# Shared pages in a recurrence without output, an identity with its own place, a new order, and a final layer norm on one engine

## The chip, the core and the metric

The kernel runs on one core of a Trainium2 chip. The metric is the device time of one execution in microseconds (us); the change is judged by the median of several executions of the kernel before and after.

## What is computed

Two layers of a block over an image stream x (512 tokens) and a context c (256 tokens), 1024 wide, in fp32. Each layer mixes a modulated input by four mixers, adds the result to the stream with a layer norm, and then does the same with a gated feed-forward. In the last layer c is only needed for the final states of its recurrence. Cut to what matters:

```python
for l in range(DEPTH):                       # 2
    last = l == DEPTH - 1
    hx, hc = xs * (1 + sc1) + sh1, cs * (1 + csc1) + csh1
    px = split(hx @ w_in[l])                 # rwkv, pool, gmlp, fnet columns
    pc = split(hc @ w_in[l][:, :RWKV_COLS]) if last else split(hc @ w_in[l])
    yc_f, sc_f = rwkv_scan(prep_c, 0, s0)    # S = S*w + (S @ -kk)(kk*a) + v k ; y = S @ r
    yc_b, sc_b = rwkv_scan(prep_c, 1, s0)
    yx_f, _ = rwkv_scan(prep_x, 0, sc_f)     # x starts from the final states of c
    yx_b, _ = rwkv_scan(prep_x, 1, sc_b)
    xs = layer_norm(ALPHA * xs + g1 * mix_out(px, yx_f, yx_b), ln1_g[l], ln1_b[l])
    xs = layer_norm(ALPHA * xs + g2 * swiglu(xs * (1 + sc2) + sh2), ln2_g[l], ln2_b[l])
    if not last:
        cs = the same two steps for c        # yc_f, yc_b are used here alone
return xs
```

## The kernel before

**Tiles.** A stream is kept in tiles of 128 tokens, x in four and c in two, each as two pages. A page is 128 partitions x 512 fp32; there are 63 of them, 12 half pages, 4 buffers (`raw`) of 512 KB in which weights land, 6 for split weights (`w`) and 8 banks of accumulators (`ps`). A matrix product is done in three matmuls of a split operand (`mm3`); so a weight that has landed is rounded on ScalarE (`w<-raw`) and its remainder taken on VectorE (`w<-raw,w`). Tensors with features on the partitions are called hT; `hT_block` makes them by transposes against the identity `idn`.

**Program and order.** `main` (L1670) writes a straight program for two branches at a time: the recurrence of one stream (`rwkv`: `rwkv_kk`, `group`, `values`, `inverse`, `scan`, `readout`) beside the output projection and feed-forward of the other (`w_out`, `ffn`, with `proj` and `proj_tile`, then a layer norm and hT). Nothing is issued while this is written. `arrange` (L560) finds the dependences, gives each instruction a due time by a backward schedule, subtracts from it the number that the table `LEAD` has for the instruction's label (one number for each label, in the order in which the labels first appear; a label is the part of the program, as `rwkv/0/x/group`), and lays the instructions out by a list scheduler (`schedule`, L404) that respects the pools and uses three more numbers (`RULES`). `emit` then issues every instruction from one line, L547, so that all rows of the profile carry that line and are told apart by the tiles' names. Each engine runs its instructions strictly in the order laid out; SP issues all DMAs, in order too.

**The lines that the change touches.**
`setup` (L682) loads the constants. `idn`, the identity and two columns of ones, comes by a DMA whose label is that of all of the setup.
`group` (L1192) prepares one direction pair of two heads in a segment of 256 tokens. Per direction it takes two pages for the rows that read the state (`AR`) and two for those that write it (`KB`), one for each of the two heads e; each page is 128 x 4 x 128. With `need_y` both column halves are used; without, which is the case for c in layer 1 alone (`start_mix(1, c, False, False)`), only the 64 columns that the state needs.
`scan` (L1377) multiplies these with the running state W.
`done` in `main` (L1759) is the final layer norm of a tile of x, after the last residual: statistics, then for the left half page two VectorE steps (x - mean) * g and * r + b, for the right half page a column nb = -mean * r on VectorE, x * r + nb on ScalarE, and on GpSimd (POOL) a multiplication by g and an addition of b; then two DMAs to the output. The table's order makes tiles 2 and 0 the last two.

Of the kernel before, what the change touches and what calls it, by code (L numbers as in the profile page):

```python
# [259 lines left out]
def analyse(ops):  # L260
# [68 lines left out]
)  # L329
RULES = {"horizon": 38406.3531, "sticky": {"scalar": 3473.0577, "tensor": 114.6915}, "cold": 1.2436167775899638e+16}  # L330


def delay(o, s):

    return LATENCY.get((o.eng, s.eng), 100.0)


def latest(ops, prio):

    n = len(ops)  # L340
# [1561 lines left out]
```

## Time and profile before

| | before |
|---|---|
| median of 3 runs | 1856.9 us (1855.26 to 1860.04) |
| the profiled execution | 1855.08 us |
| its span | 1853.3 us |
| mean granted clock of TensorE | 0.976 |
| PE busy | 1727.6 us, 93% |
| VectorE (DVE) busy | 1037.0 us, 56% |
| ScalarE (ACT) busy | 622.0 us, 34% |
| GpSimd (POOL) busy | 500.5 us, 27% |

Busy is the time in which an engine works on an instruction; a granted clock of 1.00 is 2.4 GHz, 0.50 is 1.2 GHz. The chain of waits is followed back from the last instruction to what released it at each step. Idle time of an engine matters where PE waits for it, or after PE's last matmul.

### The profile page before, as it was taken

Reading aid. Unit: us, or ns where it says so; the run is one execution under the profiler, and the core shown is the slowest. Engines: PE = TensorE matmul, PEld = TensorE weight load, DVE = VectorE, ACT = ScalarE, POOL = GpSimd, SP = SyncE. Lnnn points to the kernel's source line nnn. Section 1 sums busy time; section 2 is a strip of 40 time slices with the busy share of each in tenths; the row PEclk is TensorE's granted clock in tenths of the full one; section 3 lists DMA queues with packets and bytes.
Section 4 is the critical chain, followed back from the end, with each engine's and each line's share of the span. In section 5 each row is a group of like instructions: output and inputs, shape, how many; then the busy total and the mean of one; then the engine's idle time right before and its main releaser. Section 6 shows DMA issues by size and latency. Waiting matters only on the chain.

```text
span 1853.3 us, 33955 instructions
## 1 busy us (share of the span) xinstructions
PE 1727.6 (93%) x13896; PEld 1329.2 (72%) x13896; DVE 1037.0 (56%) x2067; ACT 622.0 (34%) x1265; POOL 500.5 (27%) x525
## 2 busy tenths in 40 slices
PE   6998889799998998999999999988979899999996
PEld 4787755588685567777787777776755788888885
DVE  3465755831253369844744456778856843443445
ACT  2455353421112124433323231564622222222220
POOL 4113531320020245600110213323416451100015
PEclk9999999799999999999999999998999999999999
DMA  8531276233463742322222223212475132333321
GB/s 308 176 114 40 83 260 222 70 115 125 143 210 124 262 155 80 125 99 84 80 92 81 84 82 119 86 57 75 138 269 183 40 112 99 99 97 112 114 80 46
DMA packets 84923, 228.93 MB, mean 124 GB/s; under 512 B 8864, under 2 KB 10272, under 8 KB 84768
## 3 DMA queue, kind: packets, MB, share of 16 engines
q1 hardware_dynamic: 84768, 226.77, 37.0%
q8 instruction: 109, 1.79, 0.4%
q14 instruction: 46, 0.38, 0.1%
HBM read 220.44 MB, written 6.29 MB: 122 GB/s over the span
## 4 chain that ended last, share of the span: by engine, by line
PE 76%; DVE 13%; DMA 4%; ACT 3%; issue 2%; POOL 1%; SPq 0%; POOLq 0%; DVEq 0%; ACTq 0%
PE ps L547 76%; DVE page L547 8%; DMA raw<-in_wm_dram 2%; DVE w L547 1%; ACT page L547 1%; POOL page L547 1%; ACT L547 1%; DVE s L547 1%; DVE NR L547 1%; ACT half L547 1%; DVE half L547 1%; DMA raw<-in_w_out_dram 1%; DMA raw<-in_w_dram 1%; DMA page<-keepM 0%; DVE Nc L547 0%
## 5 line engine op out<-in xcount | busy, mean ns | idle before, releaser
L547 PE MATMUL ps<-page,w 128*128 128x512 f32 (+1 forms) x3456 | 774.8, 377 | 25.6 <-DVE page L547 12.3
L547 PEld LDWEIGHTS ps<-page,w 128*128 128x128 f32 x3456 | 602.0, 191 | 160.2 <-DVE page L547 14.6
L547 POOL TENSOR_TENSOR page<-page 128x512 f32<-128x512 f32 (+4 forms) x250 | 324.6, 1311 | 841.8 <-DVE page L547 685.1
L547 DVE TENSOR_TENSOR w<-raw,w 128x512 fp32r<-128x512 f32 (+2 forms) x368 | 287.0, 790 | 342.7 <-PE ps L547 276.1
L547 ACT ACTIVATE w<-raw 128x512 fp32r<-128x512 f32 (+1 forms) x368 | 223.5, 624 | 515.7 <-PE ps L547 423.5
L547 PE MATMUL ps<-w,page 128*128 128x512 f32 (+2 forms) x1344 | 299.0, 369 | 4.3 <-DVE w L547 2.8
L547 PEld LDWEIGHTS ps<-w,page 128*128 128x128 f32 x1344 | 229.8, 188 | 57.3 <-issue 7.5
L547 PE MATMUL ps<-page 32*32 32x32 f32 (+2 forms) x5640 | 220.3, 221 | 25.4 <-issue 13.3
L547 PEld LDWEIGHTS ps<-page 32*32 32x32 f32 (+2 forms) x5640 | 169.0, 122 | 86.8 <-issue 43.8
L547 DVE TENSOR_TENSOR page<-ps,page 128x512 f32<-128x512 f32 x222 | 150.5, 685 | 139.9 <-PE ps L547 114.9
L547 ACT ACTIVATE page<-ps 128x256 f32<-128x256 f32 (+6 forms) x297 | 113.7, 401 | 223.8 <-PE ps L547 208.4
L547 PE MATMUL ps<-page,raw 128*128 128x256 f32 x704 | 165.0, 388 | 0.0
L547 PEld LDWEIGHTS ps<-page,raw 128*128 128x128 f32 x704 | 133.8, 193 | 26.9 <-issue 8.5
L547 PE MATMUL ps<-raw,page 128*128 128x512 f32 x240 | 113.1, 603 | 5.3 <-DVE page L547 2.4
L547 DVE TENSOR_TENSOR page<-ps,cst 64x256 f32<-64x256 f32 (+2 forms) x148 | 73.6, 513 | 21.7 <-PE ps L547 19.7
L547 PEld LDWEIGHTS ps<-raw,page 128*128 128x128 f32 x240 | 43.2, 189 | 48.4 <-issue 41.2
L547 PE MATMUL ps<-raw,sc 128*32 128x256 f32 x768 | 60.3, 408 | 17.7 <-DMA raw<-in_wm_dram 8.8
L547 ACT ACT_TABLE_LOAD x57 | 73.1, 1283 | 6.2 <-PE ps L547 4.4
L547 PE MATMUL ps<-idn,page 128*128 128x128 f32 (+1 forms) x292 | 48.8, 305 | 12.7 <-DVE page L547 10.1
L547 POOL TENSOR_TENSOR page<-page,half 64x256 f32<-64x256 f32 (+1 forms) x50 | 43.0, 860 | 65.1 <-ACT half L547 26.4
L547 POOL TENSOR_TENSOR half<-page,half 128x256 f32<-128x256 f32 x24 | 20.1, 840 | 142.7 <-DVE half L547 77.6
L547 ACT ACTIVATE half<-ps 128x256 f32<-128x256 f32 x34 | 12.9, 383 | 130.6 <-PE ps L547 130.6
(126 smaller groups left out, 1247.4 us busy)
## 6 DMA issues: line engine op xcount, KB each, us to landing
raw<-in_w_dram SPq DMA_DIRECT2D x196, 512.0 KB, 3.7
raw<-in_wm_dram SPq DMA_DIRECT2D x96, 512.0 KB, 4.6
raw<-in_win_dram SPq DMA_DIRECT2D x38, 512.0 KB, 3.6
raw<-in_w_out_dram SPq DMA_DIRECT2D x24, 512.0 KB, 4.8
page<-in_rows_dram SPq DMA_DIRECT2D x23, 256.0 KB, 5.0
page<-in_x_dram SPq DMA_DIRECT2D x16, 256.0 KB, 6.4
raw<-in_wk_dram SPq DMA_DIRECT2D x8, 384.0 KB, 6.2
page<-keepM SPq DMA_DIRECT2D x12, 256.0 KB, 4.8
```

The source lines that it names most:

```text
L547: r = getattr(getattr(nc, o.eng), meth)(*[conv(x) for x in args], **{k: conv(x) for k, x in kw.items()})
```

## The change

Three things are changed. The pages `AR` and `KB` of the two heads become one page (128 x 2 x 4 x 64) for a recurrence without output, with the column offsets set to suit. The identity's DMA gets a label of its own. The final layer norm's right half is done by two VectorE steps, as the left one, for tiles 0 and 2; tiles 1 and 3 stay as they are. Beside this every number of `LEAD` (one more than before) and of `RULES` is new. Matmuls are the same in number and shape; there are two ScalarE and four GpSimd instructions fewer, and two VectorE instructions more.

```diff
-RULES = {"horizon": 38406.3531, "sticky": {"scalar": 3473.0577, "tensor": 114.6915}, "cold": 1.2436167775899638e+16}
+RULES = {"horizon": 38909.7984, "sticky": {"scalar": 2492.3179, "tensor": 11.8601}, "cold": 2.8962643435601404e+19}
...
         idn = self.const.tile([128, 130], F32, name="idn")
+        up, nc.lab = nc.lab, ("idn",)
         nc.sync.dma_start(out=idn, in_=self.I["idn"])
+        nc.lab = up
...
-            AR.append([self.page([128, 4, 128]) for _ in range(2)])
-            KB.append([self.page([128, 4, 128]) for _ in range(2)])
+            for V_ in (AR, KB):
+                if st.need_y:
+                    V_.append([self.page([128, 4, 128]) for _ in range(2)])
+                else:
+                    t = self.page([128, 2, 4, 64])
+                    V_.append([t[:, e] for e in range(2)])
...
-                self.tt(A[:, :, ca + 1:ca + 64], nl[o, :, 1:64], c3(Pt)[o, :, 0:63], ALU.mult)
-                self.cp(A[:, :, ca:ca + 1], nl[o, :, 0:1])
+                ba = ca if st.need_y else 0
+                self.tt(A[:, :, ba + 1:ba + 64], nl[o, :, 1:64], c3(Pt)[o, :, 0:63], ALU.mult)
+                self.cp(A[:, :, ba:ba + 1], nl[o, :, 0:1])
...
             self.stt(S[0], S[0], mean, rows[0], ALU.subtract, ALU.mult)
-            self.ts(nb, mean, r, -1.0, ALU.mult, ALU.mult)
-            self.act(S[1], S[1], AF.Identity, bias=nb, scale=r)
             self.stt(S[0], S[0], r, rows[2], ALU.mult, ALU.add)
-            self.tt(S[1], S[1], rows[1], ALU.mult, self.nc.gpsimd)
-            self.tt(S[1], S[1], rows[3], ALU.add, self.nc.gpsimd)
+            if i in (0, 2):
+                self.stt(S[1], S[1], mean, rows[1], ALU.subtract, ALU.mult)
+                self.stt(S[1], S[1], r, rows[3], ALU.mult, ALU.add)
+            else:
+                self.ts(nb, mean, r, -1.0, ALU.mult, ALU.mult)
+                self.act(S[1], S[1], AF.Identity, bias=nb, scale=r)
+                self.tt(S[1], S[1], rows[1], ALU.mult, self.nc.gpsimd)
+                self.tt(S[1], S[1], rows[3], ALU.add, self.nc.gpsimd)
```

The order of the instructions at three places follows, of the kernel before and after. A row is an engine's instruction with its output and inputs by the program's names (numbers distinguish buffers), the shape, and how many of the kind follow each other.

VectorE behind w_out of layer 0 for c. `BN_STATS s_3934` (before) and `s_3831` (after) are the statistics of the last context tile; the `page<-page,mv,rs` that follows is its normalisation. Before:

```order
L547 TENSOR_TENSOR page<-ps,cst 64x256 x2
L547 TENSOR_TENSOR page<-page 128x512
L547 BN_STATS s_3934<-page 128x6 x2
L547 TENSOR_TENSOR page<-page,cst 128x512
L547 BN_AGGR mv<-s_3934 128x2
L547 TENSOR_TENSOR page<-ps,cst 64x512
L547 TENSOR_SCALAR v_3942<-mv 128x1
L547 TENSOR_REDUCE Nc<-page 128x64
L547 TENSOR_SCALAR page<-page,mv,rs 128x512
```

After:

```order
L548 TENSOR_TENSOR page<-page 128x512
L548 TENSOR_SCALAR kkn<-kkn 128x8
L548 BN_STATS s_3831<-page 128x6
L548 TENSOR_SCALAR page<-page,mv,rs 128x512 x2
L548 BN_AGGR mv<-s_3831 128x2
L548 RECIPROCAL kkn<-kkn 128x8
L548 TENSOR_SCALAR v_3847<-mv 128x1
L548 COPY page<-kkn 128x512
L548 TENSOR_SCALAR page<-page,mv,rs 128x512 x2
L548 TENSOR_TENSOR page<-page,ps 128x512
L548 TENSOR_TENSOR page<-page,half 64x4x63 x4
L548 TENSOR_TENSOR BK<-half 128x4x64 x2
L548 TENSOR_TENSOR page<-ps,cst 64x256 x2
```

The masks (`ps,cst`), the product with a constant and the reduction (`Nc`) stood ahead of the normalisation and now stand behind it.

PE where layer 0 of x ends. `ps<-w,page` are products of the projection's earlier part, `ps<-page 128x512 x72` its last part and the four residual tiles, `ps<-idn,page` the transposes to hT, `ps<-page,w 128x256` the first products of layer 1. Before:

```order
L547 MATMUL ps<-w,page 128x512 x6
L547 MATMUL ps<-page,w 128x512 x12
L547 MATMUL ps<-w,page 128x512 x12
L547 MATMUL ps<-page 128x512 x72
L547 MATMUL ps<-idn,page 128x128 x8
L547 MATMUL ps<-page,w 128x256 x12
L547 MATMUL ps<-idn,page 128x128 x16
L547 MATMUL ps<-page,w 128x256 x6
```

After:

```order
L548 MATMUL ps<-w,page 128x512 x6
L548 MATMUL ps<-page,w 128x512 x12
L548 MATMUL ps<-w,page 128x512 x15
L548 MATMUL ps<-page 128x512 x72
L548 MATMUL ps<-w,page 128x512 x3
L548 MATMUL ps<-idn,page 128x128 x24
L548 MATMUL ps<-page,w 128x256 x30
```

Three matmuls of the earlier part now stand between the last residual tile and the transposes, and the transposes and first products are no longer interleaved.

GpSimd and VectorE at the end of the program; `rs` is the reciprocal deviation of a tile. GpSimd before, then after, and VectorE after:

```order
L547 TENSOR_TENSOR rs<-v_17377,nhalf 128x1
L547 TENSOR_TENSOR page<-page 128x512 x3
L547 TENSOR_TENSOR rs<-v_17432,nhalf 128x1
L547 TENSOR_TENSOR rs<-v_17444,nhalf 128x1
L547 TENSOR_TENSOR page<-page 128x512 x4
```

```order
L548 TENSOR_TENSOR rs<-v_17369,nhalf 128x1
L548 TENSOR_TENSOR page<-page 128x512 x3
L548 TENSOR_TENSOR rs<-v_17424,nhalf 128x1
L548 TENSOR_TENSOR rs<-v_17434,nhalf 128x1
```

```order
L548 SCALAR_TENSOR_TENSOR page<-page,mv 128x512
L548 BN_STATS s_17418<-page 128x6
L548 SCALAR_TENSOR_TENSOR page<-page,mv 128x512
L548 BN_AGGR mv<-s_17418 128x2
L548 SCALAR_TENSOR_TENSOR page<-page,rs 128x512
L548 TENSOR_SCALAR v_17434<-mv 128x1
L548 SCALAR_TENSOR_TENSOR page<-page,mv 128x512 x2
L548 SCALAR_TENSOR_TENSOR page<-page,rs 128x512 x3
```

The four GpSimd steps behind the last `rs` are gone, and VectorE takes seven scalar-tensor steps after its last statistics, where there were three.

## Rows read from the trace of the kernel before

**Rows 1.** The page: busy time of each engine, and the chain that ended last.

```profile
PE 1727.6 (93%) x13896; PEld 1329.2 (72%) x13896; DVE 1037.0 (56%) x2067; ACT 622.0 (34%) x1265; POOL 500.5 (27%) x525
...
PE 76%; DVE 13%; DMA 4%; ACT 3%; issue 2%; POOL 1%; SPq 0%; POOLq 0%; DVEq 0%; ACTq 0%
```

**Rows 2.** Stretches: length, busy time (count) per engine, clock, DMA share, GB/s.

```profile
0.00:46.00 46.00, 30.90 (x177) 20.98 (x181) 17.56 (x38) 13.38 (x25) 19.67 (x50) 1.00 0.90 310
...
787.00:1145.00 358.00, 351.33 (x2344) 278.78 (x2342) 178.86 (x305) 111.36 (x209) 50.89 (x50) 1.00 0.27 90
...
1480.00:1807.00 327.00, 327.00 (x1425) 265.22 (x1424) 144.29 (x213) 88.13 (x147) 55.29 (x40) 1.00 0.32 103
...
1839.40:1853.30 13.90, 0.00 (x0) 0.00 (x0) 6.65 (x14) 1.63 (x2) 8.72 (x8) 0.68 0.25 94
```

**Rows 3.** Timeline of PE, start: start, length, instruction, [idle before, releaser].

```profile
10.40 0.99 PE L547 MATMUL ps<-idn,half 128*128 128x2 f32 x4 [2.02 <-DMA idn<-in_idn_dram]
...
16.96 1.08 PE L547 MATMUL ps<-raw,sc 128*32 128x256 f32 x8 [2.39 <-DMA raw<-in_wm_dram]
...
20.73 2.06 PE L547 MATMUL ps<-half 128*128 128x128 f32 x8
```

**Rows 4.** Timeline, 344 to 356, and the stretch behind it.

```profile
344.50 1.88 PE L547 MATMUL ps<-page 128*128 128x512 f32 x4
...
354.14 1.06 DVE L547 TENSOR_REDUCE Nc<-page 128x64 f32<-128x512 f32 x1
354.30 0.56 POOL L547 TENSOR_TENSOR rs<-v,nhalf 128x1 f32<-128x1 f32 x1 [3.65 <-DVE v L547]
...
355.11 0.54 DVE L547 TENSOR_SCALAR page<-page,mv,rs 128x512 f32<-128x512 f32 x1
...
355.71 1.97 PE L547 MATMUL ps<-idn,page 128*128 128x128 f32 x8 [5.82 <-DVE page L547]
...
352.70:362.90 10.20, 6.57 (x23) 5.55 (x24) 9.92 (x42) 5.99 (x12) 0.86 (x2) 0.50 0.01 2
```

**Rows 5.** Layer 0 to layer 1 of x: the first transposes, and two stretches.

```profile
1161.39 1.10 PE L547 MATMUL ps<-idn,page 128*128 128x128 f32 x8
...
1161.40:1183.70 22.30, 19.76 (x106) 16.58 (x105) 15.38 (x40) 9.26 (x19) 8.42 (x11) 0.85 0.11 25
1165.10:1171.90 6.80, 6.10 (x26) 5.26 (x25) 6.03 (x16) 2.66 (x6) 2.00 (x3) 0.50 0.00 0
```

**Rows 6.** Groups by form (busy us, mean ns | idle before), then timeline at 1143.

```profile
L547 DVE TENSOR_TENSOR w<-raw,w 128x512 fp32r<-128x512 f32 x352 | 277.0, 797 | 340.5 <-PE ps L547 276.1 <-ACT w L547 44.8 <-issue 18.5
L547 DVE TENSOR_TENSOR page<-ps,page 128x512 f32<-128x512 f32 x222 | 150.5, 685 | 139.9 <-PE ps L547 114.9 <-ACT page L547 12.5 <-POOL page L547 6.3
...
L547 POOL TENSOR_TENSOR page<-page 128x512 f32<-128x512 f32 x146 | 202.0, 1401 | 293.8 <-DVE page L547 212.3 <-DMA page<-in_rows_dram 39.7 <-DMA page<-in_pos_dram 16.4
...
1142.69 8.53 POOL L547 TENSOR_TENSOR page<-page 128x512 f32<-128x512 f32 x6 [19.90 <-DVE page L547]
...
1144.65 2.92 DVE L547 TENSOR_TENSOR w<-raw,w 128x512 fp32r<-128x512 f32 x2
```

**Rows 7.** Timeline of PE at 1246 to 1250, and the stretch.

```profile
1246.12 1.08 PE L547 MATMUL ps<-cst,page 128*128 128x2 f32 x8 [1.31 <-POOL page L547]
...
1250.06 1.09 PE L547 MATMUL ps<-idn,page 128*128 128x128 f32 x4 [2.87 <-DVE page L547]
...
1247.00:1253.80 6.80, 3.93 (x13) 3.30 (x13) 5.64 (x13) 3.83 (x9) 2.14 (x3) 0.50 0.00 0
```

**Rows 8.** Timeline, the end of the program.

```profile
1842.05 0.68 DVE L547 BATCH_NORM_STATS2 s<-page 128x6 f32<-128x512 f32 x1
...
1842.89 0.70 DVE L547 SCALAR_TENSOR_TENSOR page<-page,rs 128x512 f32<-128x512 f32 x1
...
1844.68 5.49 POOL L547 TENSOR_TENSOR page<-page 128x512 f32<-128x512 f32 x4
...
1844.88 1.62 DVE L547 SCALAR_TENSOR_TENSOR page<-page,rs 128x512 f32<-128x512 f32 x1
```

More of the change, by code (lines that the diff above doesn't have):

```diff
@@ L1265, in group @@
                         self.mm(pgs[e][:, j * 128 + qs[e]:j * 128 + qs[e] + nq], bk(e, j),
-                                AR[d][e][own[e], j, qs[e]:qs[e] + nq])
+                                AR[d][e][own[e], j, 0:nq])
             with nc.one():
@@ L1279, in group @@
                 self.tt(N[o, 4 * d:4 * d + 4, :], p3[o, :, ca:ca + 64], b3(o, ca, 64), ALU.mult)
-                self.tt(AR[d][e][x, :, q0:q0 + nq], p3[x, :, q0:q0 + nq], b3(x, q0, nq), ALU.mult)
+                self.tt(AR[d][e][x, :, 0:nq], p3[x, :, q0:q0 + nq], b3(x, q0, nq), ALU.mult)
                 if st.need_y:
                     self.tt(KB[d][e][o, :, cr:cr + 64], p3[o, :, cr:cr + 64], b3(o, cr, 64), ALU.mult)
-                self.cp(KB[d][e][:, :, ca:ca + 64], psK.rearrange("p (j c) -> p j c", j=4))
+                ba = ca if st.need_y else 0
+                self.cp(KB[d][e][:, :, ba:ba + 64], psK.rearrange("p (j c) -> p j c", j=4))
         st.groups[hp, i] = dict(AR=AR, KB=KB, N=N)
@@ L1383, in scan @@
         ny = st.need_y
+        cols = own if ny else [own[0]] * 2
         if first:
@@ L1396, in scan @@
                 for hp, d, e in each:
-                    self.mm(ps[e][own[e], 0, hp, d], AR[hp][d][e][:, j, own[e]], at(W, e, j)[:, hp, d], hp == d == 0, False, **kw)
+                    self.mm(ps[e][own[e], 0, hp, d], AR[hp][d][e][:, j, cols[e]], at(W, e, j)[:, hp, d], hp == d == 0, False, **kw)
                 for hp, d, e in each if ny else ():
@@ L1421, in scan @@
                     for hp, d, e in each if not last else ():
-                        self.mm(ps[e][own[e], 0, hp, d], KB[hp][d][e][:, j, own[e]], at(W, e, j)[:, hp, d], False, True, **kw)
+                        self.mm(ps[e][own[e], 0, hp, d], KB[hp][d][e][:, j, cols[e]], at(W, e, j)[:, hp, d], False, True, **kw)
                     for hp, d, e in each if ny else ():
```

47 rows, old and new, of the table LEAD are left out of this document.

## Prediction

> **What bounds the kernel now.** I read the page first: TensorE (PE) is busy 1727.6 of 1853.3 us and makes 76% of the chain that ended last, VectorE 13% [rows 1]. So a change that leaves the matmuls as they are, as this one does, can win only where PE stands still, where its clock is granted at half, or behind its last matmul. The second view is the busy time by stretch [rows 2]. It shows where nothing is to be had: 327.00 of 327.00 us busy at 1480 to 1807, 351.33 of 358.00 at 787 to 1145. The idle time lies in the first 46 us (30.90 busy, DMA share 0.90), in 139 to 371 with the recurrence of c, at 1145 to 1297 where layer 1 of x begins, in 1343 to 1480, and in the 13.90 us after the last matmul. I then followed PE's waits and the timelines there [rows 3 to 8], and put the instruction order of both kernels beside each other. Over most of the program the two orders agree; five places differ enough to be costed. The sum is made against the profiled run: 1855.1 us, of which 1853.3 are the span. The median of the three runs is 1856.9, so 1.8 us are added at the end. A measurement of this kernel tells about 0.3% from no change, 5.6 us.
>
> **Page sharing.** In layer 1 the recurrence of c takes 4 pages fewer in each of its two group calls, 8 in a segment. Number and shape of the instructions stay. That recurrence runs beside the feed-forward of x in 787 to 1145, where PE is busy 351.33 of 358.00 us [rows 2]. A page that is free earlier there lets VectorE, GpSimd and DMA run ahead of an engine that is full anyway: 0, and at most the 6.7 idle us. If that cover were gone, the wait for a page would cost a POOL or VectorE step, about 1 us at a time; I give it nothing.
>
> **The start.** PE waits 2.02 us for the identity at 10.40 and 2.39 for modulation weights at 16.96 [rows 3]. The identity now goes first in SP's queue and the two half tiles of bd and cs fifth and sixth, so that the 2.06 us of matmuls on them, which stood behind the last wait (start 20.73 [rows 3]), come first. Their price: idn, bd and cs (0.32 MB) now pass ahead of the first x tile, and the second pair of weights lands some 0.37 MB later in the queue; at the stretch's 310 GB/s that is 1.2 us. Gain 2.06 less 1.2: about -1, between -2 and +1.
>
> **The context's layer norm after w_out of layer 0** (346 to 363). The last matmul of w_out's tile starts at 344.50 and ends at 346.38, and PE stands 5.82 us before the transposes at 355.71 [rows 4]. They wait for a VectorE chain in which work of x's recurrence is mixed: five mask multiplications, a product with a constant and a reduction (354.14, 1.06), and only then the normalisation at 355.11. The new order puts all of these behind the normalisation; three short steps on kkn stay. Chain from the last matmul: residual and half-row add 0.69 each [rows 6], two statistics of 0.68 [rows 8], two normalisations of c's other tile of 0.54 [rows 4], GpSimd's rs 0.56 [rows 4] with handovers 0.3, and the steps on a few columns and kkn, 1.2 in all by my estimate from the same timeline: about 5.9 instead of 355.71 - 346.38 = 9.3. On PE some 2.5 us of work lies in between instead of 3.1, so idle falls from 6.2 to 3.4: -2.8. Behind the long gap PE's clock was granted at 0.50, its 1.2 GHz level, over 10.20 us with 6.57 us of busy time [rows 4], which is 3.3 us lost; I give back a third, -1. Bounds of this term: +1 (the shifted recurrence is late in its turn) to -7.3 (gap cut and all of the loss gone); I take -4.
>
> **From layer 0 to layer 1 of x** (1145 to 1184). This term goes the other way. Before, the residual tiles came in the order 0, 1, 3, 2, and PE passed from the last tile to the first transposes without a gap: 1161.39 [rows 5]. The work from there to the next dense block takes 22.30 us, of which PE is busy 19.76, 6.10 of that at clock 0.50 [rows 5]. So it is 16.7 us of full-speed work, 3.05 lost to the clock, 2.5 idle. After, the order is 2, 3, 0, 1, and the last three matmuls of the projection's first part (0.69 us, second half of tile 3) have moved behind all four tiles. PE's next instruction is a transpose of tiles 2 and 3. It needs the chain that only these three matmuls start: the three matmuls 0.69 and the residual 0.68, GpSimd's add 1.40, tile 3's add and tile 1's that is queued with it 1.4, two weight subtractions queued in between 0.80 each [rows 6], statistics 0.68 [rows 8], aggregation and epsilon 0.3, two statistics of tile 1 that cover GpSimd's rs 1.4, the normalisation 0.5 [rows 4]. That is 8.7, less about 0.5 where each starts before the last has ended: 8.2 us after the last tile. PE, whose queue is in order, stands for 7.5 of them. Then everything is there and the 16.7 us run densely. 8.2 + 16.7 + 3.05 for the clock - 22.3 - 0.69 (the moved matmuls, saved earlier) gives +5.0. Bounds: without any loss to the clock +1.9; with a chain of 10 and half of a stretch of 10.20 us lost, as long as that of rows 4 (5.1 us), +8.8.
>
> The trace shows what the clock does after a stall: 0.50 for 10.20 us behind the 5.82 us of idle [rows 4]. The Trainium skill (TensorE: Matmul & The Clock Gate, section "What's actually happening") has it that half speed is the default state and activity releases it; it speaks against an order that makes PE stand still once for long. By that rule this term is +5.0, without it +1.9.
>
> **The key normalisation of x's second head pair, layer 1** (1246 to 1254). PE waits 1.31 and 2.87 us, the second time for a VectorE chain, and 1247.00 to 1253.80 runs at 0.50 with 3.93 us busy [rows 7]. The new order puts 2.7 us of weight matmuls between the two steps, which closes the 2.87. The group matmuls behind them lose that cover, so some of it comes back there, at most all of it; with the clock held up over part of the stretch (2.0 us lost before, half of 3.93) I take -1.5, between -4 and 0.
>
> **The tail.** After the last matmul (1839.4) the last two tiles are normalised. GpSimd begins its four multiplications and additions at 1844.68 and needs 5.49 us, to 1850.17; the span ends 3.1 us later [rows 8]. Both are now on VectorE. Its last statistics end at 1842.73. From there stand a subtraction, an aggregation, a scaling, the epsilon, two subtractions and three scalings: seven instructions of 0.70 [rows 8], some 0.65 from start to start, and 0.2 for the small ones. 1842.73 + 7 x 0.65 + 0.2 = 1847.5; rs of the last tile (1844.7) is no longer last. The 1.62 us of one scaling at 1844.88 ran beside GpSimd's adds, which are gone. -2.7, between -1.2 (every one at 0.9) and -3.2.
>
> Elsewhere (371 to 640, and the inverse's small matmuls at 1289 to 1480, where order and weight loads stay as they were): 0, plus or minus 2.
>
> **Sum.** -1 - 4 + 5.0 - 1.5 - 2.7 = -4.2. 1855.1 - 4.2 = 1850.9, and with 1.8 for the median **1852.7**.
>
> **The rivals.**
> Larger gain: the stall at the layer boundary comes without loss to the clock (+1.9) and the gap at 355.71 takes its slow stretch with it (-7.3): -1 - 7.3 + 1.9 - 1.5 - 2.7 = -10.6, 1846. For it: both slow stretches follow idle times of several us [rows 4, 7], and one of them is shortened. Against: the new stall is longer than any of them.
> Only the tail: the order's gains and losses cancel, -2.7, 1854. For it: PE's idle time is spread over many small waits, and what one gives the next takes.
> Slower: the stall at the boundary costs its upper bound. Its place is the wait of tile 3's transposes, its price 8.8: two weight subtractions took 2.92 us at 1144.65, beside GpSimd's row of adds (1142.69, 8.53 us), instead of 1.6 [rows 6], and with such a pair in it the chain is near 10. If the context's norm then gives nothing and the key normalisation's gap only moves, with the start at +1: 1 + 0 + 8.8 + 0 - 2.7 = +7.1, 1864. It is slower by over 0.3% once the boundary costs 8.3 with the other order terms at nothing. The Trainium skill (SBUF — State Buffer, section "SBUF: two separate sides") names a port pair that VectorE and GpSimd take in turn, each for a whole instruction; the 2.92 us agree, and by that rule the chain is 10, not 8.2, since GpSimd adds beside it.
> That the change doesn't do what it says: the tail is sure to move, since no GpSimd add is left behind it.
>
> **How the numbers follow.** The sum with its spread (1848 to 1857): 0.50, of which 0.20 lies below 1851.3 and 0.30 within 0.3%. Larger gain 0.23, faster. Only the tail 0.10, same. Slower 0.17. So faster 0.43, same 0.40, slower 0.17. The range goes from 1843 to 1863: it takes in most of the larger gain and leaves out about half of the slower case and little below.
>
> **What would show it.** GpSimd has nothing after its last rs, and the span ends about 8 us after the last VectorE statistics and 11 after the last matmul. The transposes of c start some 6 us behind w_out's last matmul, and the clock of 352 to 363 tells what that is worth. At the layer boundary PE's longest single wait, 7 to 8 us, stands before a transpose and is put down to VectorE; if it is under 3, the larger gain is right. At the start no wait for the identity is left. The sum is wrong if a new wait for weights shows in 1290 to 1480, where DMA has little to spare, or if the matmuls' total at full clock changes.

## The result and the profile after

| | before | after |
|---|---|---|
| median | 1857.07 us (1855.26 to 1860.04) | 1830.96 us (1828.23 to 1836.04) |
| the profiled execution, its span | 1855.08, 1853.3 us | 1830.23, 1828.5 us |
| PE busy | 1727.6 us | 1720.1 us |
| PE idle up to its last matmul | 111.8 us | 96.7 us |
| from the last matmul to the end | 13.9 us | 11.7 us |

The ratio of after to before is 0.9873, with a 95% interval from 0.9846 to 0.99: 19 to 29 us faster; the medians differ by 26. I had forecast 4 us, with 1843 as the range's lower end. The sign was right, the size wrong by a factor of six.

The page of the kernel after, busy time and chain (before: [rows 1]):

```profile
PE 1720.1 (94%) x13896; PEld 1325.7 (73%) x13896; DVE 1028.1 (56%) x2069; ACT 613.9 (34%) x1259; POOL 493.3 (27%) x521
...
PE 79%; DVE 10%; DMA 6%; issue 2%; ACT 2%; POOL 1%; SPq 0%; DVEq 0%; ACTq 0%; POOLq 0%
```

VectorE's share of the chain fell from 13% to 10%. The same 13896 matmuls take 7.5 us less of busy time and stand in 15.1 us less of idle time; the end adds 2.2. These three are the 24.8 us between the two spans.

To see where the 24.8 us arose, I put the matmuls of both traces side by side by their place in the program and read, at several of them, by how much the kernel after is ahead of the kernel before (us; the differences are those of the unrounded times):

| where (before, after, us) | ahead | gained in the stretch | what it is |
|---|---|---|---|
| 256.4, 253.4 | 3.0 | +3.0 | start, first recurrence |
| 391.2, 371.7 | 19.5 | +16.5 | c's readout, w_out and layer norm |
| 468.5, 455.2 | 13.3 | -6.1 | x's recurrence, put off |
| 693.6, 678.1 | 15.5 | +2.2 | |
| 1154.8, 1130.0 | 24.8 | +9.3 | feed-forward of x, layer 0, beside c's recurrence without output |
| 1191.0, 1169.6 | 21.4 | -3.4 | layer 0 to layer 1 of x |
| 1314.5, 1285.9 | 28.7 | +7.3 | key norm, first groups of layer 1 |
| 1489.4, 1466.6 | 22.8 | -5.9 | scan of layer 1, modulation weights |
| 1839.4, 1816.8 | 22.6 | -0.2 | |
| end | 24.8 | +2.2 | tail |

**The context's norm.** PE and its waits in the kernel before, ahead of the gap that [rows 4] show (timeline: start, length, instruction, idle time before it and what ended it; then the window that begins there, columns as in [rows 2]):

```profile
323.91 0.60 PE L547 MATMUL ps<-idn,page 128*64 128x128 f32 x4 [0.68 <-issue]
...
326.33 0.70 PE L547 MATMUL ps<-page,cst 128*128 128x256 f32 x2 [0.50 <-ACT half L547]
...
329.92 1.22 PE L547 MATMUL ps<-page,sp 128*128 128x256 f32 x2 [1.65 <-DVE page L547]
...
332.72 2.08 PE L547 MATMUL ps<-page 128*128 128x512 f32 x2 [0.73 <-DVE page L547]
```

```profile
328.80:339.00 10.20, 8.36 (x32) 4.55 (x34) 4.53 (x15) 4.58 (x16) 3.43 (x8) 0.50 0.19 59
```

The same steps in the kernel after:

```profile
317.66 0.70 PE L548 MATMUL ps<-page,cst 128*128 128x256 f32 x2
...
318.92 0.70 PE L548 MATMUL ps<-page,sp 128*128 128x256 f32 x2
...
320.75 9.61 PE L548 MATMUL ps<-page 128*128 128x512 f32 x22
...
335.13 4.18 PE L548 MATMUL ps<-idn,page 128*128 128x128 f32 x20 [2.94 <-DVE page L548]
```

```profile
335.50:338.90 3.40, 3.39 (x17) 2.99 (x16) 3.31 (x7) 2.29 (x6) 1.92 (x4) 0.50 0.00 0
```

Before, readout and w_out of c are cut up by six waits, 4.85 us in all (the four rows, and 0.69 and 0.60 for modulation weights), and 10.20 us run at the clock's lower level, 1.2 GHz. After, w_out runs through without a wait; the gap before the transposes is 2.94 instead of 5.82, and the slow stretch behind it 3.40 instead of 10.20. The waits for modulation weights are not gone: they stand ahead of these rows in the kernel after, 1.37 us at 315.82 and 0.62 at 317.09.

Of the 16.5 us gained here, 6.1 go back at once. Before, PE is full in the stretch that follows; after, the recurrence of x that was put off falls into it, with 308 matmuls more, 2.2 us more of busy time and 4.0 of idle time. Before, and then after:

```profile
391.20:468.50 77.30, 77.30 (x715) 64.29 (x714) 15.04 (x35) 9.89 (x27) 0.91 (x3) 1.00 0.35 117
```

```profile
371.70:455.20 83.50, 79.48 (x1023) 64.59 (x1022) 32.10 (x69) 20.09 (x53) 4.08 (x7) 1.00 0.30 102
```

**The feed-forward of x.** The stretch up to the last residual tile, before and after, nearly the same matmuls:

```profile
708.00:1161.40 453.40, 436.98 (x2839) 351.75 (x2837) 267.18 (x453) 150.35 (x286) 107.50 (x103) 0.99 0.27 92
```

```profile
694.00:1137.00 443.00, 433.29 (x2832) 351.18 (x2830) 257.26 (x441) 142.71 (x280) 104.41 (x94) 0.99 0.28 90
```

10.4 us less, of which idle time is 6.7 (16.4 to 9.7) and busy time 3.7. The seven matmuls fewer are 128x512 products at the window's start and make 1.9 of the 3.7. The clock doesn't make the rest: it stands at 1.2 GHz for 6.8 us in both, near the window's start. Behind that, at a clock of 1.00 (740.00 to 1161.40 before, 725.00 to 1137.00 after), PE is busy for 410.45 and 407.62 us, and the largest group, 1008 products of one shape, is (busy us, mean ns | idle time before them; before, then after):

```profile
L547 PE MATMUL ps<-page,w 128*128 128x512 f32 x1008 | 249.2, 397 | 6.0 <-DVE w L547 3.7 <-DVE page L547 2.3
L548 PE MATMUL ps<-page,w 128*128 128x512 f32 x1008 | 244.6, 396 | 1.9 <-DVE w L548 1.7 <-DVE page L548 0.2
```

So the same products at the same clock count as busy for 4.6 us less. In the trace such a product lasts 0.39 us and the next one starts 0.23 us behind it (1135.66 and 1135.89 in the kernel after), so a pause of up to 0.16 us between two of them counts as busy. The idle time fell at the waits for pages, and not at those for the split weights `w` (over the whole stretch: us in total, times, longest; before, then after):

```profile
PE ps L547 <- DVE w L547: 5.8, 8, 1.4
PE ps L547 <- POOL page L547: 4.4, 5, 1.4
...
PE ps L548 <- DVE w L548: 6.4, 7, 2.3
PE ps L548 <- POOL page L548: 1.9, 1, 1.9
```

The waits for pages from VectorE fell from 3.1 to 0.7 us as well.

**Layer 0 to layer 1 of x.** The first transposes and two stretches after (before: [rows 5]):

```profile
1144.16 4.52 PE L548 MATMUL ps<-idn,page 128*128 128x128 f32 x23 [7.31 <-DVE page L548]
```

```profile
1141.00:1147.80 6.80, 3.64 (x17) 3.65 (x18) 6.10 (x18) 3.13 (x7) 1.94 (x3) 0.50 0.25 80
1144.10:1166.50 22.40, 21.47 (x121) 18.97 (x122) 15.16 (x37) 13.40 (x26) 8.62 (x11) 0.92 0.25 78
```

**Layer 1.** The next two stretches of the table, before and then after:

```profile
1191.00:1314.50 123.50, 111.27 (x1253) 90.07 (x1252) 93.15 (x210) 72.01 (x158) 34.63 (x41) 0.94 0.26 84
...
1314.50:1489.40 174.90, 154.42 (x2037) 105.74 (x2036) 125.08 (x275) 54.11 (x127) 78.38 (x71) 0.97 0.50 162
```

```profile
1169.60:1285.90 116.30, 109.13 (x1253) 87.72 (x1252) 90.01 (x211) 68.95 (x155) 34.31 (x41) 0.99 0.30 92
...
1285.90:1466.60 180.70, 160.19 (x2037) 110.35 (x2036) 124.78 (x275) 55.12 (x128) 77.11 (x72) 0.92 0.49 160
```

In the first, 5.1 us of idle time are gained, and the clock is 0.99 instead of 0.94. In the second, idle time is the same (20.48 and 20.51), and the 5.8 us that are lost are all busy time: the clock is 0.92 instead of 0.97. After, PE stands here once for 2.08 and once for 3.91 us, and 10.20 us run at 1.2 GHz around the end of the first wait and again behind the second (timeline, then two windows):

```profile
1336.63 3.39 PE L548 MATMUL ps<-page 32*32 32x32 f32 x124 [2.08 <-issue]
...
1351.87 0.44 PE L548 MATMUL ps<-page 32*32 32x32 f32 x29 [3.91 <-issue]
```

```profile
1335.60:1345.80 10.20, 8.17 (x268) 5.79 (x268) 2.67 (x6) 1.52 (x6) 2.52 (x2) 0.50 0.50 176
1352.70:1362.90 10.20, 9.99 (x188) 5.99 (x182) 2.61 (x5) 4.64 (x11) 0.00 (x0) 0.50 0.70 225
```

**The tail.** The last steps on GpSimd and VectorE, and the stretch (before: [rows 8] and the last of [rows 2]):

```profile
1822.07 0.99 POOL L548 TENSOR_TENSOR rs<-v,nhalf 128x1 f32<-128x1 f32 x1 [1.72 <-DVE v L548]
1823.24 2.06 DVE L548 SCALAR_TENSOR_TENSOR page<-page,rs 128x512 f32<-128x512 f32 x3
```

```profile
1816.80:1828.50 11.70, 0.00 (x0) 0.00 (x0) 8.50 (x17) 0.00 (x0) 3.85 (x4) 0.65 0.30 112
```

GpSimd has nothing behind its last `rs`. VectorE ends at 1825.30, 8.5 us after the last matmul, and the span 3.2 us later.

### The profile page after: what moved, and what is told of

It reads as the page before. It is cut to its first block, busy times and chain, and to the rows that moved or that the text cites. A ratio compares the mean times of both kernels' runs of the same rounds, so it can differ in the third digit from the quotient of the medians.

```text
span 1828.5 us, 33950 instructions
## 1 busy us (share of the span) xinstructions
PE 1720.1 (94%) x13896; PEld 1325.7 (73%) x13896; DVE 1028.1 (56%) x2069; ACT 613.9 (34%) x1259; POOL 493.3 (27%) x521
## 4 chain that ended last, share of the span: by engine, by line
PE 79%; DVE 10%; DMA 6%; issue 2%; ACT 2%; POOL 1%; SPq 0%; DVEq 0%; ACTq 0%; POOLq 0%
PE ps L548 79%; DVE page L548 6%; DMA raw<-in_wm_dram 3%; DVE w L548 1%; DMA raw<-in_w_dram 1%; DVE s L548 1%; ACT page L548 1%; DMA raw<-in_wk_dram 1%; POOL page L548 1%; DMA raw<-in_w_out_dram 1%; ACT w L548 0%; ACT L548 0%; DVE BK L548 0%; ACT half L548 0%; DVE NR L548 0%
## 5 line engine op out<-in xcount | busy, mean ns | idle before, releaser
L548 PE MATMUL ps<-page,w 128*128 128x512 f32 (+1 forms) x3456 | 764.6, 376 | 18.0 <-DVE w L548 6.4
L548 POOL TENSOR_TENSOR page<-page 128x512 f32<-128x512 f32 (+4 forms) x246 | 317.4, 1304 | 895.7 <-DVE page L548 599.4
L548 DVE TENSOR_TENSOR w<-raw,w 128x512 fp32r<-128x512 f32 (+2 forms) x368 | 276.8, 766 | 311.2 <-PE ps L548 231.4
L548 ACT ACTIVATE page<-ps 64x128 f32<-64x128 f32 (+6 forms) x297 | 113.8, 402 | 203.8 <-PE ps L548 197.5
L548 PE MATMUL ps<-raw,sc 128*32 128x256 f32 x768 | 65.0, 430 | 15.0 <-DMA raw<-in_wm_dram 11.4
```

What stands on the lines that cost most here:

```text
L548: r = getattr(getattr(nc, o.eng), meth)(*[conv(x) for x in args], **{k: conv(x) for k, x in kw.items()})
```

## The experiments

Two orders can be computed for the changed program, one from the new numbers and one from those of before. Several kernels below are put together from both: the first so many instructions of one order, then those of the other that are not yet there up to a place, then the rest; the place where one order takes over from the other is called a seam. All were timed in three rounds beside the kernel before, whose median was 1853.87, 1856.88 or 1858.09 us there; so ratios to that kernel are compared, with their 95% intervals, and not times. The kernel after has 0.9873 [0.9846, 0.99] on this scale.

**Which part of the change.** `old_numbers` is the changed program with the numbers of before (`LEAD0`, `RULES0`; the identity counts under its old label there):

```diff
         q = nr.setdefault(o.lab, len(nr))
-        at[o.i] -= LEAD[q] if q < len(LEAD) else 0
-    return schedule(ops, tag, caps, at, **RULES)[0]
+        at[o.i] -= LEAD0[q] if q < len(LEAD0) else 0
+    return schedule(ops, tag, caps, at, **RULES0)[0]
```

> The changed program (shared pages, tail on VectorE, own label for the identity) laid out by the table of numbers of before. Theory: the numbers made the gain, and the code only gives the tail, 2.2 us by the two traces: 1854.7 us. Rival: the shared pages let the feed-forward of x run ahead and give the 8 us that PE gained between 787 and 1135: 1846 to 1848 us, with PE idle of 1 us or less in that stretch instead of 6.

1885.95 us, 1.0178 [1.0137, 1.022]: slower than before. Both expectations missed. `no_sharing` is the other corner, the new numbers with two pages per pair of heads:

```diff
-                    t = self.page([128, 2, 4, 64])
-                    V_.append([t[:, e] for e in range(2)])
+                    V_.append([self.page([128, 4, 128]) for _ in range(2)])
```

> The changed kernel with a page of its own for each head again, new numbers kept. Theory: nothing hangs on the pages, 1829 to 1833 us, and PE stays full beside the feed-forward of x (idle under 1.5 us there). Rival: the pages carry the feed-forward stretch, and without them 6 to 8 us come back: 1837 to 1839 us.

1854.72 us, 1.0005 [0.9986, 1.0024]: none of the gain is left, and both expectations missed again. Up to some 700 us its trace runs with that of after; then it falls behind by 26 us up to the place where after stands at 1122. The stretch of the feed-forward in `no_sharing`, and PE's waits in it (us in total, times, longest):

```profile
694.00:1162.00 468.00, 442.06 (x2832) 353.02 (x2831) 254.08 (x440) 145.68 (x283) 101.87 (x95) 0.99 0.25 86
```

```profile
PE ps L548 <- DVE w L548: 10.4, 15, 1.4
PE ps L548 <- DVE page L548: 6.8, 7, 2.7
PE ps L548 <- ACT w L548: 3.2, 5, 1.3
```

and in `old_numbers`:

```profile
703.00:1187.00 484.00, 447.84 (x2834) 351.09 (x2833) 260.31 (x447) 149.91 (x287) 102.01 (x92) 0.99 0.26 86
```

```profile
PE ps L576 <- DVE w L576: 11.7, 21, 1.4
PE ps L576 <- ACT w L576: 7.6, 12, 1.4
```

The same work takes 443.0 us in after, 453.4 in before, 468.0 and 484.0 here; PE waits for the split weights (`w`) for 13.6 us in `no_sharing` and 19.3 in `old_numbers`, against 6.4 in after, so these come later. (Both have some 13.6 us at 1.2 GHz in this stretch, where before and after have 6.8; so part of their longer busy time, at most 3.4 us, is the clock's.) Is that a lack of pages in the run, or the order that the planner lays out when it counts them? `plan_apart` shares the pages, but its order is planned as if they were apart; while `schedule` runs, each half of a shared page has a name of its own:

```diff
+            if nm in SHARED:
+                nm = "%s/%d" % (nm, a.offset % list(a.ap)[0][0] // 256)
+                tag[nm] = tag[a.name]
```

> The changed program with its shared pages, laid out as if the heads' pages were still apart: the order of no_sharing, on shared pages. Theory: a page's supply costs nothing by itself; what the changed kernel loses without sharing is the order that the same numbers give when the scheduler sees other free pages, so 1853 to 1857 us as no_sharing. Rival: engines wait for pages in the run itself, and with shared pages under the same order the time falls towards 1831 us.

1855.06 us, 0.9998 [0.998, 1.0015], and the stretch as in `no_sharing`:

```profile
694.00:1162.00 468.00, 441.63 (x2829) 352.33 (x2827) 256.61 (x442) 145.12 (x281) 104.15 (x98) 0.99 0.26 86
```

In the traces of `plan_apart` and `no_sharing` every engine runs the same sequence, and `plan_apart` differs from after in its order alone. So under this order the eight free pages cost or bring nothing that these intervals can tell while the program runs, and the order alone makes the 24 us. The pages act through the planner: with the same numbers it lays out another order where eight more pages are to be had.

**How far such a table carries.** `jitter` moves every number of the table by 1%, up and down in turn:

```diff
-LEAD = (5803, 163341, -3776, 3034, ...
+LEAD = (5745, 164974, -3738, 3064, ...
```

> The changed program with every number of its table 1% up or down in turn. Theory: the numbers are a fit to this one program, and the 24 us that page sharing seems worth are what any disturbance of the fit costs: 1845 to 1865 us. Rival: the table is robust, and it is the eight pages that the order needs: within 4 us of 1831.

2121.86 us, 1.1421 [1.1396, 1.1447], far outside of all that was expected. PE's longest sum of waits in `jitter`:

```profile
PE ps L523 <- ACT w L523: 75.7, 72, 4.0
```

The numbers are a fit to one program. This also says how to read the two corners above: they measure what becomes of a fit when the program under it changes, and not what the pages are worth. Apart from the kernel before, no numbers fitted to the program without sharing were tried, so it stays open whether a new fit of it would reach 1831 too.

**The context's stretch.** `ctx_old` is the kernel after with the order of before between about 256 and 520 us, and `ctx_alone` the reverse, the kernel before (no sharing, old tail) with the new order there. The first is put together like this:

```diff
+def splice(parts):
+    done, out = set(), []
+    for name, stop in (("new", 1220), ("old", 2180), ("new", None)):
+        out += [o for o in parts[name][:stop] if o.i not in done]
+        done = {o.i for o in out}
+    return out
```

> The changed kernel, with the order of before only in the stretch from some 256 to 520 us (end of the context's recurrence, its w_out and layer norm, x's inverse beside the context's feed-forward); new order before and behind. Theory: this stretch holds the largest part of the gain, PE was 2.5 us ahead at its start and 14 at its end, so about 10 to 11 us come back: 1841 to 1842 us, with the gaps at 324 to 333 and before the context's transposes (5.8 us) back, and the clock at half behind them. Rival: what the stretch gains is given back later by work that it only put off, the time stays within 3 us of 1831.

1846.67 us, 0.9953 [0.9934, 0.9973]: 15 us of the gain go, more than either expectation. The waits and the long slow stretch are back, as the timeline and a window of `ctx_old` show:

```profile
330.37 0.70 PE L576 MATMUL ps<-page,sp 128*128 128x256 f32 x2 [1.72 <-DVE page L576]
...
353.81 1.97 PE L576 MATMUL ps<-idn,page 128*128 128x128 f32 x8 [5.82 <-DVE page L576]
```

```profile
349.20:359.40 10.20, 4.94 (x19) 4.27 (x20) 9.99 (x38) 4.38 (x9) 0.87 (x2) 0.50 0.05 13
```

> The kernel before (pages apart, old tail) in its own order, but with the new order in the stretch from some 256 to 530 us (end of the context's recurrence, its w_out and layer norm, its feed-forward beside x's inverse). Theory: this order pays by itself, as much as taking it away cost, 10 to 16 us: 1838 to 1844 us, without the gaps at 324 to 333 and the one of 5.8 us before the context's transposes. Rival: it pays only with the stretch behind it that was fitted to it, and the time stays within 4 us of 1854.

1861.8 us, 1.0035 [1.0021, 1.0049]. At 500 us it is 10 to 11 us ahead of before, but the seam between the orders then makes PE wait once for a weight that is issued too late, and that decides the total, so the run says nothing of the rest:

```profile
544.42 4.16 PE L576 MATMUL ps<-page,raw 128*128 128x256 f32 x9 [13.23 <-DMA raw<-in_w_dram]
```

So the seam was put later, to about 640 us, in `ctx_alone2`:

```diff
-    for name, stop in (('old', 1220), ('new', 2180), ('old', None)):
+    for name, stop in (('old', 1220), ('new', 2620), ('old', None)):
```

> As ctx_alone, with the seam behind the new stretch moved on, from some 530 to some 640 us, since in ctx_alone PE waited 13.2 us at 544 for a weight that the two orders load at different places. Theory: the new order of the context's stretch pays by itself: PE 10 to 12 us ahead of before at 500 us, and 1842 to 1847 us in the end. Rival: it pays only together with the numbers for what follows; PE is ahead at 500 us, but the time stays within 4 us of 1856.

1847.16 us beside 1858.09, 0.9945 [0.9927, 0.9963]: 10.9 us gained on the kernel before by the order of this stretch alone. PE's wait in it is that of after:

```profile
336.17 4.21 PE L576 MATMUL ps<-idn,page 128*128 128x128 f32 x20 [2.93 <-DVE page L576]
```

This is the one part of the order that was run alone, and it gains by itself, on code without sharing and with the old tail.

**The layer boundary.** `mend` moves by hand what the prediction named: the three late matmuls with their VectorE and GpSimd steps ahead of the first tile, the chain of tile 3 ahead of tile 1's, the two weight subtractions behind the norm (C is the projection's first part, T % i, N % i and H % i the residual, norm and transposes of tile i, W6 the weight).

```diff
+    move("tensor", [(C, 27)], (T % 2, 0))
+    move("vector", [(C, 10)], (T % 2, 0))
+    move("gpsimd", [(C, 3)], (T % 2, 0))
+    move("vector", [(T % 3, 2), (N % 3, 1), (N % 3, 2), (N % 3, 3)], (N % 0, 1))
+    move("gpsimd", [(N % 3, 0)], (T % 1, 0))
+    move("vector", [(N % 3, 4), (N % 3, 5)], (N % 0, 4))
+    move("vector", [(W6, 0), (W6, 1)], (H % 3, 2))
```

> The changed kernel with three hand moves at the end of layer 0 of x: the three matmuls of the projection's earlier part back ahead of the residual tiles (and the two additions behind them), tile 3's statistics and normalisation ahead of tile 1's on VectorE, the two weight subtractions behind the layer norm. Theory: PE's wait of 7.3 us before the transposes falls to 2 or 3, the time by 4 to 5: 1826 to 1827 us. Rival: another step of the layer norm is as late (tile 1's), the wait stays above 5 us and the time within 2 us of 1831.

1833.8 us, 0.9886 [0.9853, 0.992]: not faster. The wait of 7.31 is split in three in `mend`, 8.98 in all:

```profile
1142.60 1.62 PE L576 MATMUL ps<-idn,page 128*128 128x128 f32 x10 [2.36 <-DVE page L576]
1147.77 2.96 PE L576 MATMUL ps<-idn,page 128*128 128x128 f32 x13 [3.55 <-DVE page L576]
1154.31 5.03 PE L576 MATMUL ps<-page,w 128*128 128x256 f32 x29 [3.07 <-POOL page L576]
```

The longest of them ends with the normalisation at 1147.17, by the moves that of tile 1, which I had put behind. `bound_old` puts the whole order of before there (about 1110 to 1215 us), with the new one on both sides:

```diff
+    for name, stop in (('new', 4420), ('old', 4780), ('new', None)):
```

> The changed kernel with the old numbers' order at the end of layer 0 of x alone (some 1110 to 1215 us): residual tiles in the order 0, 1, 3, 2, three matmuls of the earlier part back in their place, transposes and first products interleaved. Theory: PE's wait of 7.3 us goes, 3 to 5 us come off: 1826 to 1828 us. Rival: the wait only splits into several (as in mend, 2.4 + 3.6 + 3.1), and the time stays within 2 us of 1831.

1832.24 us, 0.9871 [0.9846, 0.9897]: no gain either. The order of before, which passed here without a wait at 1161.39 [rows 5], and had 2.5 us of idle time in the 22.30 that follow, now waits 0.62, 4.49, 0.96, 0.28, 0.83 and 0.46, 7.6 us together:

```profile
1140.49 1.75 PE L576 MATMUL ps<-idn,page 128*128 128x128 f32 x7 [4.49 <-DVE page L576]
```

So the order at this place alone doesn't decide the loss: with either order PE waits here for VectorE, in one piece or in several, once the program ahead of it is the new one. Whether that lies in what comes ahead or in the seam can't be told from this run.

**The 5.9 us handed back in layer 1.** `mend_l1` is `mend` with the order of before between about 1226 and 1420 us.

```diff
-    for name, stop in (('new', None),):
+    for name, stop in (('new', 5020), ('old', 5740), ('new', None)):
```

> mend with the order of before in the stretch from some 1226 to 1420 us (x's inverse, scan and the modulation's weights in layer 1), where the changed kernel lost 5 us against before (two stretches of 10 us at half the clock). Theory: the order makes that loss, and 3 to 5 us come off: 1822 to 1824 us. Rival: the stretch is set by the weight DMAs (0.78 to 0.83 of the DMA engines busy), the gain elsewhere only arrives there early and waits, and the time stays within 1 us of mend.

1834.37 us, 0.9883 [0.9852, 0.9913], as `mend`. At 1311 to 1375 PE is busy for 52.89 us at a clock of 0.84 in `mend` and for 53.28 at 0.87 in `mend_l1`.

The rival's time came. Its cause, the landing of weights, is not shown by that: in the kernel after the two long waits here are "issue", behind which the profile shows no releaser. What holds PE there stays open.

**The tail and the start.** `old_tail` is the kernel after with the final norm of before; `start_old` has the order of before up to about 236 us.

```diff
-            if i in (0, 2):
-                self.stt(S[1], S[1], mean, rows[1], ALU.subtract, ALU.mult)
-                self.stt(S[1], S[1], r, rows[3], ALU.mult, ALU.add)
-            else:
...
+            self.tt(S[1], S[1], rows[1], ALU.mult, self.nc.gpsimd)
+            self.tt(S[1], S[1], rows[3], ALU.add, self.nc.gpsimd)
```

> The changed kernel with the final layer norm of before for all four tiles (right half on ScalarE and GpSimd). Theory: the time behind the last matmul grows from 11.7 to 13.9 us, 1833.2 us, nothing else moves. Rival: the last outputs' transfers set the end either way, and the time stays at 1831 us.

1831.87 us, 0.9881 [0.9843, 0.992], which can't be told from after. The traces tell: the end comes 14.3 us after the last matmul, not 11.7, and GpSimd has its row again, in `old_tail`:

```profile
1821.78 5.49 POOL L548 TENSOR_TENSOR page<-page 128x512 f32<-128x512 f32 x4
```

```diff
+    for name, stop in (('old', 1100), ('new', None)):
```

> The changed kernel with the old numbers' order up to some 236 us (identity behind the first x tiles in SP's queue, half tiles late), new order behind. Theory: 2 to 4 us of the gain come from this stretch, most of it not in the first 40 us: 1833 to 1835 us. Rival: the loading at the start hides any order, and the time is 1831 within 1 us.

1835.55 us, 0.9887 [0.9866, 0.9908]. By the medians not resolved either; in the trace 3.3 us of the lead are gone at 256 us and 5.4 at the last matmul.

No version beat the kernel after.

## Why the prediction was wrong

**"Over most of the program the two orders agree; five places differ enough to be costed."** This is the step that failed. Against the sum, 20.6 us of gain were missing in the profiled run: 9.3 in the feed-forward, 6.4 at the context's norm with what was handed back, 5.8 at the key normalisation, 2.0 at the start and 1.6 at the boundary, less 4.5 elsewhere and in the tail. Most of it lies in stretches that I held to be the same. I had read it from PE's order, and even that is not the same: at 256.4, 693.6, 1191.0, 1314.5 and 1489.4 us of the table PE has the same work behind it in both kernels, but in another sequence. Between 693.6 and 1154.8 us before, the longest sequence that both traces have in common, by names and shapes, takes in 80% of PE's matmuls, 71% of VectorE's instructions and 48% of SP's transfers. When PE may do its work is set by the rows of VectorE, ScalarE, GpSimd and SP, and those had moved too. "Elsewhere: 0, plus or minus 2" covered stretches that came out at +2.2, -6.1 and -5.9.

**The context's norm: 4 forecast, 16.5 gained up to 391 us, 10.4 of it kept.** The step that I costed was right in kind and size: idle 6.2 to 3.4 forecast, 5.82 to 2.94 for its largest wait. The clock, of which I gave back 1, gave more: the slow stretch behind the gap went from 10.20 to 3.40 us, the rival of the larger gain. What I missed lies 20 us earlier. VectorE's work on x's second pair of heads, which I saw move behind c's normalisation, moved behind c's readout and w_out too. The waits at 323.9 to 332.7 went, and with them the slow 10.20 us of 328.80 to 339.00. Of these waits 1.65 and 0.73 us were for VectorE; what ended the shorter ones was not tested one by one. I had read that part of the timeline and took it as unchanged. The lower bound of -7.3 is also no sum of its parts: -2.8 for the gap and -3.3 for all of the clock's loss make -6.1, so the rival of the larger gain stands at -9.4 and 1847.5, not at -10.6 and 1846. `ctx_old` (15 us) and `ctx_alone2` (10.9 us) show that the term is real and stands by itself.

The windows bear on what the Trainium skill says of the clock (TensorE: Matmul & The Clock Gate, section "What's actually happening": half speed is the default, activity releases it). The trace agrees in both directions: without the gaps at 324 to 356 two stretches of 10.20 us at 1.2 GHz shrink to one of 3.40, and in layer 1, at an equal sum of idle time, longer gaps (3.91 us at most instead of 2.88) go with 27 us at 1.2 GHz instead of 10 and with 5.8 us more of busy time.

**Page sharing: 0, "an engine that is full anyway", at most 6.7.** Here two steps failed. A PE that is 98% busy was taken as bound by itself; the stretch fell by 10.4 us, 3.7 of them out of its busy time, and 1008 equal products at full clock are busy for 244.6 us instead of 249.2. Busy time is no floor. And I asked what a free page is worth to the run (`plan_apart`: nothing) but not what it does to the order that a planner with 63 pages lays out (`no_sharing`, `old_numbers`: 24 and 32 us against the kernel that the numbers were fitted to).

**The start: -1 forecast, -3.0 at 256 us,** but not for my reason. No wait for the identity is left, as forecast, yet the first matmul comes 0.65 us later and the modulation weights cost 3.45 instead of 2.39:

```profile
7.10 2.04 PE L548 MATMUL ps<-half 128*128 128x128 f32 x8 [7.10 <-DMA half<-in_cs_dram]
...
16.45 1.08 PE L548 MATMUL ps<-raw,sc 128*32 128x256 f32 x8 [3.45 <-DMA raw<-in_wm_dram]
```

The price was sized right (1.06 for 1.2). What the forecast left out is the first matmul, which waits for `cs`, and the clock: the kernel after runs at 1.2 GHz from 14.60 to 28.20, where its first 18 products of `w` take 6.15 us; before, 14 of them take 3.51 at 26.32:

```profile
14.60:28.20 13.60, 10.06 (x47) 6.36 (x48) 6.50 (x10) 2.91 (x5) 6.09 (x5) 0.50 1.04 403
24.56 6.15 PE L548 MATMUL ps<-page,w 128*128 128x512 f32 x18
```

The clock of 1.00 that [rows 2] give for the start of the kernel before is not borne out by its own rows: eight modulation products take 1.08 us at 16.96 [rows 3], 0.70 at 24.85 and 0.64 at 29.76, by which it too ran slow up to about 25. At 40 us the lead is 0.2; the rest comes between 78 and 150, where I had costed nothing.

**The layer boundary: +5.0 forecast, +3.4 in the stretch.** The wait was right: 7.5 forecast, 7.31 measured, before a transpose and put down to VectorE. The clock cost less than the 3.05 that I took over from before: the slow 6.80 us have 3.64 of busy time, 1.8 lost, and 3.2 us of the wait lie in them. But the new order at this place is not all that the loss hangs on: in `bound_old`, with the old order there, the waits are 7.6 us. My account, the three late matmuls and tile 3's chain, describes the wait, but taking it away doesn't end it: `mend` moved all of it ahead, and PE waited longest for what had been put behind instead.

**The key normalisation: -1.5 forecast, -7.3 in its stretch.** The wait of 1.31 went, but that of 2.87 is gone by name only: PE now stands between the same two steps for 2.55 us, in the very weight matmuls that were to close the 2.87, for a weight that ScalarE has not rounded yet:

```profile
1225.24 2.46 PE L548 MATMUL ps<-page,w 128*128 128x512 f32 x6 [2.55 <-ACT w L548]
```

So the 2.87 was not closed, and 4.18 us of idle time became 2.55. The rest of the gain lies elsewhere in the stretch: a wait that I had not costed, 3.50 us at 1271.84, shrank to 1.18, and the clock rose from 0.94 to 0.99, of which I had given back half for one slow stretch alone. Some of the 7.3 returned at 1315 to 1490.

**The tail: -2.7 forecast, -2.2 between the spans, -2.6 against `old_tail`.** Right by each of its steps: 8.1 us from the last matmul to VectorE's end forecast, 8.5 measured, and nothing left on GpSimd.

**The rivals.** The larger gain (1846) named the right mechanism, a slow stretch that goes with its gap, at one place where it acted at three. "Slower" had its place at the boundary; its wait came and was paid for several times over upstream. The pair of weight subtractions that was to stretch the chain to 10 us took 0.67 and 0.63 us (1141.06 and 1141.77), with no GpSimd addition beside it, so the price of such a pair was not put to a test.

## What to carry to other kernels

Where a change replaces the order of a whole program, compare the order of every engine that the bottleneck waits for, not of the bottleneck alone; and list every wait of over half a microsecond with what it waits for before saying that a stretch stays as it is. A short wait in a full stretch is worth more than its idle time when the clock falls behind it, so count slow stretches beside waits. A table of numbers that sets an order is fitted to one program: a small edit to the program or the table can cost more than either is worth (here 24 to 290 us), so taking one part of such a change away without fitting again measures the broken fit too.

## What the runs showed of the hardware

The busy time of PE holds more than its work. The same 1008 products at a granted clock of 1.00 are busy for 249.2 us in the kernel before and 244.6 in the kernel after, where 6.0 and 1.9 us of idle time stand before them. Over the whole feed-forward the busy time is 433.3, 437.0, 442.1 and 447.8 us (x2832 to x2839) in after, before, `no_sharing` and `old_numbers`, and idle time grows with it, 9.7, 16.4, 25.9 and 36.2; the last two have 13.6 us at 1.2 GHz instead of 6.8, so the clock makes at most 3.4 us of what they are longer. And the clock fell to 1.2 GHz for 10.20 us not only behind one long wait, the 5.82 us of [rows 4], but also at 328.80, behind four waits of 0.50 to 0.69 us since 323.2 and within a fifth, of 1.65.
